# Strassen's seven products for two token chunks of an MLP's up-projection, and a down-projection by pairs of blocks

## The chip, the core and the metric

The kernel runs on one core of one Trainium2 chip. The metric is the device time of one execution in microseconds (us). Three runs of the kernel before took 1270.1, 1270.6 and 1271.15 us; the median is 1270.6.

## The reference

One layer of a hybrid decoder trunk for 1024 prompt tokens and 32 sample tokens of width 1024, in fp32. The first sub-layer (a mixer of gated spatial mixing, a gated linear recurrence and a convolution, between one input and one output projection) is not touched by the change. The second is a squared-ReLU MLP between two normalisations:

```python
h = _rmsnorm(x, g_pre_mlp[l]) * (1.0 + sc2) + sh2
y = jnp.square(jax.nn.relu(h @ w_up[l])) @ w_down[l]
x = x + gt2 * _rmsnorm(y, g_post_mlp[l])
```

`w_up` is 1024 x 4096 and `w_down` 4096 x 1024.

## The kernel before, in words

**Layout.** Features lie on the 128 partitions, tokens on the free axis. The 1056 tokens are `NCH` = 3 chunks of `CW` = 352 columns. `h2[c]` (filled by `after_mix`, L1487) holds the MLP's input of chunk c as 8 blocks of 128 features, each as a high and a low part in the fp32r format (hi is the rounded value, lo the rest). A weight block is split in the same way, so each product of a weight block with a block of tokens takes three matmuls: hi x hi, hi x lo, lo x hi (`product`, L344; `product8`, L354, does eight blocks of the contraction, 24 matmuls).

**The MLP.** The 32 output blocks of the up-projection are done four at a time, in eight steps j = 0 to 7 (loop at L1657). In a step, for each of four blocks f and three chunks, `up_group` (L1539) runs 24 matmuls into a PSUM tile, then ScalarE's ReLU (`relu`) and Square (`ah`, the high part), VectorE's square (`rsq`) and its residue (`al`, the low part). Then the down-projection of these four blocks: for each of eight output blocks m and three chunks `down_group` (L1554) runs 12 matmuls (four blocks of the contraction) into a PSUM tile, and VectorE adds it to the accumulator `acc`. So a step has 288 + 288 matmuls. In step 0 chunks 0 and 1 go through both projections before chunk 2, whose `h2` is ready last, and ScalarE copies instead of VectorE adding. In step 7 `last_down_group` (L1570) cuts the tokens into other groups, and `after_ff` (L1602) normalises and stores each.

**Weights.** `jobs` (from L283) lists the weight blocks of 512 KB in order of use. `fetch` (L300) allocates one of three `raw` tiles and issues its DMA on SyncE's queue; `split_next` (L307) has ScalarE write the high part (`whi`, 1024 columns) and VectorE the low part (`wlo`); `weights` (L336) hands out the oldest and splits ahead until two are ready. In the MLP there are three pairs of hi and lo tiles.

**Buffers.** PSUM has eight banks: three in the pool `pm` (L177; `pm_tile`, L365, all products so far) and five in `pb` (L178). SBUF tiles of 1056 columns come from `ep`, 17 of them (tag "e"; `full` and `e3`); eight are the accumulators, one per chunk and three m (the ninth piece is in `e2`), and eight the activations `ah` and `al` of a step. Each accumulator group of three for m = 6, 7 has a free third place.

**Order.** Every engine works through its own queue in the order in which the program issues. The order is written by hand: loops issue matmul groups, and `step(t)` (L224) between them lets generator tasks (`add_task`) issue the work of other stages, kind by kind, as long as a credit of time per engine (`Metered`, L85, with prices by operation) is left; `finish` (L249) issues what is left of all tasks.

Of the kernel before, what the change touches and what calls it, by code (L numbers as in the profile page):

```python
# [26 lines left out]
T_GROUP = 3.57  # L27
# [132 lines left out]
def trunk_kernel(ctx: ExitStack, tc: tile.TileContext, xT, cT, wada0, wada, vec, cst, msk, win, wout, wup,  # L160
# [5 lines left out]
    PE = Metered(nc.tensor, pe_price, credit, "pe", plan)  # L166
# [40 lines left out]
    def rs(name):  # L207
        return sp.tile([128, 512], F32, tag="rs", name=name)
# [40 lines left out]
    def finish():  # L249
        while any(queues.values()):  # L250
            step(T_GROUP / 2)
# [23 lines left out]
    jobs = []  # L275
# [10 lines left out]
    for cs in ((0, 1), (2,)):  # L286
        for f in range(4):
            jobs.append((wup[f], [128, 8, 128]))
        for m2 in range(4):
            jobs.append((wdn[0, m2], [128, 2, 4, 128]))  # L290
    for j in range(1, 8):
        for f in range(4):
            jobs.append((wup[4 * j + f], [128, 8, 128]))
        for m2 in range(4):
            jobs.append((wdn[j, m2], [128, 2, 4, 128]))

    homes = {}
    raws = []
# [1 line left out]
    def fetch():  # L300
        if jobs:
            src, shape = jobs.pop(0)
            raw = wp.tile(shape, F32, tag="raw", name="raw", bufs=3)
            SP.dma_start(out=raw, in_=src)
            raws.append((raw, shape))

    def split_next(later=False):  # L307
# [57 lines left out]
    def pm_tile():  # L365
        return pm.tile([128, CW], F32, tag="m", name="pmt")
# [231 lines left out]
    def hc(name):  # L598
        return hp.tile([128, 8, CW], F32, tag="c", name=name)
# [236 lines left out]
    def ch(t, c):  # L836
        return t[:, c * CW:(c + 1) * CW]
# [696 lines left out]


    acc = [None] * NCH
    homes[n_w[0] + len(raws) + len(jobs) - 1] = hc

    def up_group(w, a, c, j):  # L1539
        ps = pm_tile()  # L1540
        product8(ps, w, lambda k: (h2[c][0][:, k, :], h2[c][1][:, k, :]))
        ah, al = a
        t = rs("relu")[:, 0:CW]
        ACT.activation(out=t, in_=ps, func=AF.Relu)
        s2 = rs("rsq")[:, 0:CW]
        if j == 0:
            ACT.activation(out=s2, in_=t, func=AF.Square)
        else:
            DVE.tensor_tensor(out=s2, in0=t, in1=t, op=ALU.mult)
        ACT.activation(out=r(ch(ah, c)), in_=t, func=AF.Square)  # L1550
        DVE.tensor_tensor(out=r(ch(al, c)), in0=s2, in1=ch(ah, c), op=ALU.subtract)
        step(T_GROUP / STEPS)

    def down_group(w, mm, m, acts, c, j):  # L1554
        hi, lo = w
        ps = pm_tile()
        product(ps, (lambda k: hi[:, mm, k, :], lambda k: lo[:, mm, k, :]),
                lambda k: (ch(acts[k][0], c), ch(acts[k][1], c)), 4)
        a = acc[c][1](m)
        if j == 0:  # L1560
            ACT.copy(out=a, in_=ps)
        else:
            DVE.tensor_tensor(out=a, in0=a, in1=ps, op=ALU.add)
        step(T_GROUP / 2)


    CUT = 96
# [86 lines left out]

    put_off, rest = [], []

    for j in range(8):  # L1657
        acts = [(full("ah"), full("al")) for f in range(4)]
        if j == 0:
            for cs in ((0, 1), (2,)):  # L1660
                ws = {}
                for c in cs:
                    while h2[c] is None:
                        step(T_GROUP / 2)
                    for f in (3, 0, 1, 2) if c == 1 else range(4):
                        if c != 1:
                            ws[f] = weights()
                        up_group(ws[f], acts[f], c, j)
                if cs[0] == 0:
                    for c in range(NCH):  # L1670
                        acc[c] = blocks_of([(extra if (c, kk) == (2, 2) else e3)("acc") for kk in range(3)])
                for m2 in range(4):
                    w = weights()
                    for mm in range(2):
                        for c in cs:
                            down_group(w, mm, 2 * m2 + mm, acts, c, j)
            finish()
        else:
            for f in range(4):
# [3 lines left out]
        if j == 0:  # L1683
            continue
        if j < 7:
            for m2 in range(4):
                w = weights()
                for mm in range(2):
                    for c in range(NCH):
                        down_group(w, mm, 2 * m2 + mm, acts, c, j)  # L1690
        else:
            ws = []
            x1 = hc("x1")
            SP.dma_start(out=x1, in_=x1d[1])
            x1_last = hc("x1l")[:, 6:8, :]
            SP.dma_start(out=x1_last, in_=x1d[0, :, 6:8, :])
            tots = hc("tots")
            for g, parts in enumerate(GROUPS):
                tot = tots[:, 2 * g:2 * g + 2, :].rearrange("p a n -> p (a n)")[:, 0:sum(b - a for c, a, b in parts)]
                for m2 in range(4):  # L1700
                    if len(ws) < 4:
                        ws.append(weights())
                    for mm in range(2):
# [109 lines left out]
```

## Time and profile before

| | |
|---|---|
| runs, median (lowest to highest) | 1270.6 us (1270.1 to 1271.15) |
| profiled execution, own time | 1270.47 us |
| its span, first to last instruction | 1268.7 us |
| mean granted TensorE clock | 0.991 |
| TensorE busy | 1237.8 us, 8770 recorded matmuls |
| VectorE busy | 719.3 us |
| ScalarE busy | 488.4 us |
| GpSimd busy | 63.0 us |

Times in rows of the profile are in us unless a mean is marked ns. PE is TensorE, DVE VectorE, ACT ScalarE, POOL GpSimd, SP SyncE. A group's row gives what is written and read, the count, busy time and the mean of one in ns, and the idle time ahead of it with what ended that. All instructions are recorded at line L113, inside the wrapper that prices them, so groups are told apart by their tiles: `pmt` is a PSUM tile of a product, `h20hi` the high part of h2 in chunk 0, `ah`/`al` the activations, `whi`/`wlo` the split weights. Some matmul records are missing (of 768 matmuls with `ah` and `whi`, 744 are there), so counts of matmuls are taken from the code. The shown duration of a matmul (about 0.32 us) includes its pipeline; the pace is the distance between starts.

### The profile page before, as it was taken

What the parts mean: (1) busy time and instruction counts of PE and PEld (TensorE: products, weight loads), DVE (VectorE), ACT (ScalarE), POOL (GpSimd) and SP (SyncE); (2) the same over time, 40 slices, a digit from 0 to 9 for tenths busy, and PEclk for the clock granted to TensorE, in tenths of its full rate; (3) what the DMA queues carried; (4) which work ended last, traced back from release to release, by engine and by line L of the source; (5) the groups of instructions that cost most, each with busy time, mean ns of one, the idle gap of its engine ahead of it and who ended that gap; (6) DMA issues with size and microseconds to landing.
All of it is one profiled execution on the core that took longest, in us unless ns stands there. A gap on an engine that the chain in (4) does not pass through costs nothing.

```text
span 1268.7 us, 20674 instructions
## 1 busy us (share of the span) xinstructions
PE 1237.8 (98%) x8770; PEld 1194.8 (94%) x8770; DVE 719.3 (57%) x1096; ACT 488.4 (38%) x882; POOL 63.0 (5%) x107
## 2 busy tenths in 40 slices
PE   9999999999899999999999999999999999999995
PEld 7888889999899999899999999999999999999994
DVE  5799899688758768763333343333433333343366
ACT  6513464684764745555320321311311311312333
POOL 0000020211010011100000000000000000000001
PEclk9999999999999999999999999999999999999997
DMA  9568401111111467233211111111111110111218
GB/s 364 175 211 275 167 26 55 40 59 47 34 42 48 158 174 224 68 124 117 67 50 34 50 51 50 34 50 51 46 38 51 50 51 34 51 51 43 81 18 209
DMA packets 39245, 113.23 MB, mean 89 GB/s; under 512 B 9952, under 2 KB 12160, under 8 KB 39024
## 3 DMA queue, kind: packets, MB, share of 16 engines
q1 hardware_dynamic: 34832, 99.22, 22.8%
q0 software_dynamic: 4320, 12.68, 4.3%
q8 instruction: 69, 1.13, 0.3%
q14 instruction: 24, 0.20, 0.0%
HBM read 101.75 MB, written 10.14 MB: 88 GB/s over the span
## 4 chain that ended last, share of the span: by engine, by line
PE 81%; DVE 9%; ACT 6%; issue 1%; DMA 1%; POOL 1%; ACTq 0%; DVEq 0%; POOLq 0%
PE pmt L113 74%; PE stps L113 2%; PE adaps L113 1%; DVE acc L113 1%; DVE vf L113 1%; DMA o<-in_xT 1%; DVE q L113 1%; ACT vf L113 1%; ACT K L113 1%; PE sc L113 1%; DVE wlo L113 1%; PE pmt L736 1%; ACT whi L113 1%; DVE y L113 1%; DVE R L113 0%
## 5 line engine op out<-in xcount | busy, mean ns | idle before, releaser
L113 PE MATMUL pmt<-ah,whi 128*128 128x352 f32 (+2 forms) x744 | 241.4, 324 | 0.5 <-ACT acc L113 0.5
L113 PE MATMUL pmt<-al,whi 128*128 128x352 f32 (+2 forms) x744 | 240.3, 323 | 0.3
L113 PE MATMUL pmt<-ah,wlo 128*128 128x352 f32 (+2 forms) x744 | 240.2, 323 | 0.0
L113 ACT CAST whi<-raw 128x1024 fp32r<-128x1024 f32 (+2 forms) x113 | 114.2, 1013 | 262.2 <-PE pmt L113 260.1
L113 DVE TENSOR_TENSOR acc<-acc,pmt 128x352 f32<-128x352 f32 (+2 forms) x176 | 87.8, 503 | 167.6 <-PE pmt L113 167.6
L113 DVE TENSOR_TENSOR wlo<-raw,whi 128x1024 fp32r<-128x1024 f32 (+2 forms) x113 | 134.9, 1196 | 69.6 <-ACT whi L113 69.6
L113 DVE TENSOR_TENSOR rsq<-relu 128x352 f32<-128x352 f32 x84 | 44.2, 526 | 188.8 <-ACT relu L113 188.8
L113 PEld LDWEIGHTS pmt<-ah,whi 128*128 128x128 f32 x744 | 139.9, 188 | 2.0 <-ACT acc L113 0.8
L113 PEld LDWEIGHTS pmt<-al,whi 128*128 128x128 f32 x744 | 140.0, 188 | 1.6 <-DVE al L113 0.8
L113 PEld LDWEIGHTS pmt<-ah,wlo 128*128 128x128 f32 x744 | 140.0, 188 | 0.4
L113 ACT ACTIVATE relu<-pmt 128x352 f32<-128x352 f32 x96 | 44.6, 465 | 235.6 <-PE pmt L113 235.6
L113 PE MATMUL pmt<-h22hi,whi 128*128 128x352 f32 x256 | 82.5, 322 | 0.0
L113 PE MATMUL pmt<-h22hi,wlo 128*128 128x352 f32 x256 | 82.5, 322 | 0.0
L113 PE MATMUL pmt<-h22lo,whi 128*128 128x352 f32 x256 | 82.3, 322 | 0.0
L113 DVE SCALAR_TENSOR_TENSOR cva<-cvx,vec_t,cva 128x1024 f32<-128x1024 f32 x60 | 77.7, 1295 | 1.2
L113 PE MATMUL pmt<-h21lo,whi 128*128 128x352 f32 x232 | 74.7, 322 | 2.4 <-DVE h21lo L113 2.4
L113 PE MATMUL pmt<-h21hi,whi 128*128 128x352 f32 x232 | 75.2, 324 | 0.0
L113 PE MATMUL pmt<-h20hi,whi 128*128 128x352 f32 x232 | 74.8, 322 | 0.0
L113 PE MATMUL pmt<-h21hi,wlo 128*128 128x352 f32 x232 | 74.8, 322 | 0.0
L113 PE MATMUL pmt<-h20hi,wlo 128*128 128x352 f32 x232 | 74.7, 322 | 0.0
L113 PE MATMUL pmt<-h20lo,whi 128*128 128x352 f32 x232 | 74.6, 322 | 0.0
L113 DVE TENSOR_TENSOR al<-rsq,ah 128x352 fp32r<-128x352 f32 x96 | 50.4, 525 | 23.8 <-ACT ah L113 14.7
(361 smaller groups left out, 2694.8 us busy)
## 6 DMA issues: line engine op xcount, KB each, us to landing
rawada<-in_wada SPq DMA_DIRECT2D x48, 512.0 KB, 8.2
raw<-in_wup SPq DMA_DIRECT2D x36, 512.0 KB, 3.4
raw<-in_wdn SPq DMA_DIRECT2D x36, 512.0 KB, 3.4
raw<-in_win SPq DMA_DIRECT2D x22, 512.0 KB, 3.6
raw<-in_wout SPq DMA_DIRECT2D x20, 512.0 KB, 3.5
x<-in_xT SPq DMA_DIRECT2D x6, 528.0 KB, 6.9
o<-in_xT POOLq DMA_DIRECT2D x6, 528.0 KB, 7.3
x1d<-o POOLq DMA_DIRECT2D x6, 528.0 KB, 7.6
```

What stands on the lines that cost most here:

```text
L113: return f(**kw)
L736: nc.tensor.matmul(out=pss[m, c], lhsT=r(w_first[m][i % 2][:, k, :]), rhs=r(h[c][i // 2][:, k, :]), start=k == i == 0, stop=k == 7 and i == 2)
```

## The change

**Strassen (Winograd's form).** From the third pair of output blocks on (p = 2 is still plain, p = 3 to 15 are not), the up-projection works on pairs of output blocks. For chunks 0 and 1 the product of a 2 x 2 matrix of weight halves W(i, j) (i: half of the contraction, four blocks of 128; j: output block of the pair) with a 2 x 2 matrix of token halves is made by seven products of 12 matmuls (`part`, half depth) in place of eight. Chunk 2 keeps its 24 matmuls for each output block. This takes:

- sums of h, made once: `sums_of_h` in two parts (tasks during the end of step 0 and during p = 2) and `first_sum_of_h` (during the down-projection of p = 2, into the places of half of chunk 1's h2), each split into high and low part;
- sums of weights, for each pair: T12 and T34, two sums of 512 columns each, written by VectorE into PSUM tiles of `pb`, then cast by ScalarE and completed by VectorE (`begin_next`). Each is handled as one more weight block: a pair uses T12, W2, T34 and W1, and two blocks of down weights;
- three accumulators A, B, C in PSUM, of which partial values are taken between products (`pair_up`): three ScalarE copies and five VectorE additions with places in `acc`'s free thirds.

**Down-projection by pairs.** For p = 2 to 13 the down-projection follows each pair: 24 groups of six matmuls (two blocks of the contraction, the pair's second output block first, chunks in the order 2, 1, 0), each added to `acc` by VectorE (`down_pair`). A block of down weights now holds four m and two blocks of the contraction and is loaded by two DMAs. The last four blocks (pairs 14 and 15) go through `last_down_group` as before.

**Order of splits.** The splitting of weights is cut into `chores`, of which one is issued behind each product or group; `weight` hands out a block and begins the next.

```diff
-    for j in range(1, 8):
...
+    for p in range(2, 16):
+        for f in range(2):
+            jobs.append((wup[2 * p + f], [128, 8, 128]))
+        if p < 14:
+            for m4 in range(2):
+                jobs.append(([wdn[p // 2, 2 * m4 + i, :, :, p % 2 * 2:p % 2 * 2 + 2, :] for i in range(2)],
+                             [128, 4, 2, 128]))
+    for m2 in range(4):
+        jobs.append((wdn[7, m2], [128, 2, 4, 128]))
...
+    def sums_of_h(ks):
+        TT = DVE.tensor_tensor
+        (h0, l0), (h1, l1) = h2[0], h2[1]
+        for k in ks:
+            if k < 2:
+                ts = [full("s").rearrange("p (a n) -> p a n", n=CW) if k + i == 0 else extra("s") for i in range(2)]
+            else:
+                ts = [full("s").rearrange("p (a n) -> p a n", n=CW) for i in range(2)]
+            a, b, c, d = (*(spare(i) for i in range(3)), rstd_tile("d"))
+            TT(out=a, in0=h1[:, k, :], in1=l1[:, k, :], op=ALU.add)
+            TT(out=b, in0=h1[:, 4 + k, :], in1=l1[:, 4 + k, :], op=ALU.add)
+            yield
+            TT(out=c, in0=h0[:, k, :], in1=l0[:, k, :], op=ALU.add)
+            TT(out=b, in0=a, in1=b, op=ALU.add)
+            yield
+            TT(out=a, in0=c, in1=a, op=ALU.subtract)
+            TT(out=c, in0=b, in1=c, op=ALU.subtract)
+            yield
+            TT(out=d, in0=h0[:, 4 + k, :], in1=l0[:, 4 + k, :], op=ALU.add)
+            TT(out=d, in0=d, in1=c, op=ALU.subtract)
+            yield
+            at = [ts[i // 3][:, i % 3, :] for i in range(6)]
+            for i, x in enumerate((c, a, d)):
+                ACT.copy(out=r(at[2 * i]), in_=x)
+            yield 1.0
+            for i, x in enumerate((c, a, d)):
+                TT(out=r(at[2 * i + 1]), in0=x, in1=at[2 * i], op=ALU.subtract)
+                S[2 + i, k] = at[2 * i], at[2 * i + 1]
+            yield
...
+    KINDS = ["plain"] * 2 + (["T12", "W2", "T34", "W1"] + ["plain"] * 2) * 11 + ["T12", "W2", "T34", "W1"] * 2
...
+    def chore():
+        if chores:
+            chores.pop(0)()
+        while jobs and len(raws) + len(cur) < 3:
+            fetch()
...
+    def begin_next():
+        while chores:
+            chore()
+        kind = KINDS[begun[0]] if begun[0] < len(KINDS) else "plain"
+        begun[0] += 1
+        if kind == "plain":
+            if not raws:
+                fetch()
+            raw, shape = raws.pop(0)
+            cur["plain"] = raw
+            hi, lo = slot(shape)
+            split_of(hi, lo, raw, lambda: cur.pop("plain"))
+            ready.append((hi, lo))
+            return
+        W = lambda i, j: cur[j][:, 4 * i:4 * i + 4, :]
+        if kind in ("W1", "W2"):
+            hi, lo = slot([128, 8, 128])
+            split_of(hi, lo, cur[int(kind[1]) - 1], (lambda: cur.pop(0)) if kind == "W1" else None)
+            ready.append((hi, lo))
+            return
+        hi, lo = slot([128, 8, 128])
+        half = lambda t, i: t[:, 4 * i:4 * i + 4, :]
+        if kind == "T12":
+            while len(raws) < 2:
+                fetch()
+            cur[0], cur[1] = raws.pop(0)[0], raws.pop(0)[0]
+            ts = cur["T"] = [pb.tile([128, 4, 128], F32, tag="b", name="T") for i in range(2)]
+            DVE.tensor_tensor(out=ts[0], in0=W(0, 1), in1=W(0, 0), op=ALU.subtract)
+            DVE.tensor_tensor(out=ts[1], in0=W(1, 1), in1=ts[0], op=ALU.subtract)
+        else:
+            ts = [pb.tile([128, 4, 128], F32, tag="b", name="T"), cur.pop("T")[1]]
+            DVE.tensor_tensor(out=ts[0], in0=W(1, 1), in1=W(0, 1), op=ALU.subtract)
+            DVE.tensor_tensor(out=ts[1], in0=W(1, 0), in1=ts[1], op=ALU.subtract)
+            cur.pop(1)
+        def casts():
+            for i in range(2):
+                ACT.copy(out=r(half(hi, i)), in_=ts[i])
+        def rest():
+            for i in range(2):
+                DVE.tensor_tensor(out=r(half(lo, i)), in0=ts[i], in1=half(hi, i), op=ALU.subtract)
+        chores.extend((casts, rest))
+        ready.append((hi, lo))
+    def weight(more=True):
+        w = ready.pop(0)
+        if more:
+            begin_next()
+        return w
...
+        def part(ps, w, x, first=True):
+            hi, lo = w
+            for k in range(4):
+                xh, xl = x(k)
+                a, b = first and k == 0, k == 3
+                PE.matmul(out=ps, lhsT=r(hi[:, k, :]), rhs=r(xh), start=a, stop=False, skip_group_check=True)
+                PE.matmul(out=ps, lhsT=r(hi[:, k, :]), rhs=r(xl), start=False, stop=False, skip_group_check=True)
+                PE.matmul(out=ps, lhsT=r(lo[:, k, :]), rhs=r(xh), start=False, stop=b, skip_group_check=True)
...
+        def squares(*ts):
+            s2s = []
+            for t, f, c in ts:
+                s2s.append(rs("rsq")[:, 0:CW])
+                DVE.tensor_tensor(out=s2s[-1], in0=t, in1=t, op=ALU.mult)
+                ACT.activation(out=r(ch(acts[f][0], c)), in_=t, func=AF.Square)
+            for s2, (t, f, c) in zip(s2s, ts):
+                DVE.tensor_tensor(out=r(ch(acts[f][1], c)), in0=s2, in1=ch(acts[f][0], c), op=ALU.subtract)
...
+        p5 = p1 = spare(0)
+        p6, c12, c22 = spare(1), spare(2), rstd_tile("c22")
+        T12 = weight()
+        C = pm_tile()
+        part(C, half(T12, 0), sum_(1))
+        ACT.copy(out=p5, in_=C)
+        go_on()
+        B = pb.tile([128, CW], F32, tag="b", name="pmt2")
+        part(B, half(T12, 1), sum_(2))
+        ACT.copy(out=p6, in_=B)
+        go_on()
+        W2 = weight()
+        part(C, half(W2, 1), sum_(4), False)
+        add(c12, C, p6)
+        go_on()
+        A = pb.tile([128, CW], F32, tag="b", name="pmt2")
+        def third():
+            part(B, half(T34, 0), sum_(3), False)
+            add(c22, B, p5)
+            go_on()
+        def first():
+            part(A, half(W1, 0), of_h(0, 0))
+            add(c12, A, c12)
+            add(c22, A, c22)
+            ACT.copy(out=p1, in_=A)
+            squares((relu(c12, c12), 1, 0), (relu(c22, c22), 1, 1))
+            go_on()
+        def fourth():
+            part(B, half(T34, 1), of_h(1, 1), False)
+        def c21():
+            add(p1, B, p1)
+            squares((relu(p1, p1), 0, 1))
+        if last:
+            T34 = weight(False)
+            third()
+            chunk2(1, W2)
+            begin_next()
+            fourth()
+            go_on()
+            W1 = weight()
+            acts[0] = full("ah"), full("al")
+            first()
+            c21()
+            chunk2(0, W1)
+        else:
+            chunk2(1, W2)
+            T34 = weight()
+            third()
+            W1 = weight(False)
+            acts[0] = full("ah"), full("al")
+            first()
+            fourth()
+            begin_next()
+            c21()
+            go_on()
+            chunk2(0, W1)
+        part(A, half(W1, 1), of_h(0, 1), False)
+        squares((relu(A, rs("relu")[:, 0:CW]), 0, 0))
+        go_on()
...
+    def down_pair(w, mm, m, acts, c):
+        hi, lo = w
+        ps = pm_tile()
+        product(ps, (lambda k: hi[:, mm, 1 - k, :], lambda k: lo[:, mm, 1 - k, :]),
+                lambda k: (ch(acts[1 - k][0], c), ch(acts[1 - k][1], c)), 2)
+        a = acc[c][1](m)
+        DVE.tensor_tensor(out=a, in0=a, in1=ps, op=ALU.add)
+        step(T_GROUP / 4)
...
+    for p in range(2, 14):
+        acts = {}
+        if p == 2:
+            acts = {f: (full("ah"), full("al")) for f in range(2)}
+            add_task("conv", sums_of_h((2, 3)))
+            for f in range(2):
+                w = weight()
+                for c in range(NCH):
+                    up_group(w, acts[f], c, 1)
+                    chore()
+            add_task("conv", first_sum_of_h())
+        else:
+            pair_up(acts, False)
+        for m4 in range(2):
+            w = weight()
+            for mm in range(4):
+                for c in (2, 1, 0):
+                    down_pair(w, mm, 4 * m4 + mm, acts, c)
+                    chore()
+        if p == 2:
             finish()
-        else:
-            for f in range(4):
-                w = weights()
-                for c in range(NCH):
-                    up_group(w, acts[f], c, j)
-        if j == 0:
-            continue
-        if j < 7:
-            for m2 in range(4):
-                w = weights()
-                for mm in range(2):
-                    for c in range(NCH):
-                        down_group(w, mm, 2 * m2 + mm, acts, c, j)
-        else:
-            ws = []
-            x1 = hc("x1")
-            SP.dma_start(out=x1, in_=x1d[1])
-            x1_last = hc("x1l")[:, 6:8, :]
-            SP.dma_start(out=x1_last, in_=x1d[0, :, 6:8, :])
-            tots = hc("tots")
-            for g, parts in enumerate(GROUPS):
-                tot = tots[:, 2 * g:2 * g + 2, :].rearrange("p a n -> p (a n)")[:, 0:sum(b - a for c, a, b in parts)]
-                for m2 in range(4):
-                    if len(ws) < 4:
-                        ws.append(weights())
-                    for mm in range(2):
-                        last_down_group(ws[m2], mm, 2 * m2 + mm, acts, parts, tot)
-                add_task("first" if parts[0][0] == 1 else "recur", after_ff(parts, tot, parts[0][0] == 1))
+    acts, more = {}, {}
+    pair_up(acts, False)
+    pair_up(more, True)
...
```

More of the change, by code (lines that the diff above doesn't have):

```diff
@@ L303, in fetch @@
             raw = wp.tile(shape, F32, tag="raw", name="raw", bufs=3)
-            SP.dma_start(out=raw, in_=src)
+            if isinstance(src, list):
+                for i, x in enumerate(src):
+                    SP.dma_start(out=raw[:, 2 * i:2 * i + 2], in_=x)
+            else:
+                SP.dma_start(out=raw, in_=src)
             raws.append((raw, shape))
@@ L1536, in trunk_kernel @@
     acc = [None] * NCH
-    homes[n_w[0] + len(raws) + len(jobs) - 1] = hc
     def up_group(w, a, c, j):
@@ L1564, in down_group, with spare @@
         step(T_GROUP / 2)
+    S = {}
+    def spare(c):
+        return acc[c][1](8)
+    def sums_of_h(ks):
[27 more added lines that the diff above has]
+            yield
@@ new lines, in first_sum_of_h @@
+    def first_sum_of_h():
+        TT = DVE.tensor_tensor
+        h1, l1 = h2[1]
+        for k in range(4):
+            a, b = spare(k % 2), rstd_tile("d")
+            TT(out=a, in0=h1[:, k, :], in1=l1[:, k, :], op=ALU.add)
+            TT(out=b, in0=h1[:, 4 + k, :], in1=l1[:, 4 + k, :], op=ALU.add)
+            yield
+            TT(out=a, in0=a, in1=b, op=ALU.add)
+            ACT.copy(out=r(h1[:, k, :]), in_=a)
+            yield 0.5
+            TT(out=r(l1[:, k, :]), in0=a, in1=h1[:, k, :], op=ALU.subtract)
+            S[1, k] = h1[:, k, :], l1[:, k, :]
+            yield
@@ new lines, in trunk_kernel, with slot, split_of @@
+    chores = []
+    cur = {}
+    begun = [0]
+    KINDS = ["plain"] * 2 + (["T12", "W2", "T34", "W1"] + ["plain"] * 2) * 11 + ["T12", "W2", "T34", "W1"] * 2
+    def slot(shape):
+        n_w[0] += 1
+        pool = wpools[n_w[0] % len(wpools)]
+        return [pool.tile(shape, F32, tag=f"w{x}", name=f"w{x}") for x in ("hi", "lo")]
+    def chore():
[3 more added lines that the diff above has]
+            fetch()
+    def split_of(hi, lo, src, done=None):
+        ACT.copy(out=r(hi), in_=src)
+        def rest():
+            DVE.tensor_tensor(out=r(lo), in0=src, in1=hi, op=ALU.subtract)
+            if done:
+                done()
+        chores.append(rest)
@@ new lines, in begin_next, with rest @@
+    def begin_next():
[35 more added lines that the diff above has]
+                ACT.copy(out=r(half(hi, i)), in_=ts[i])
+        def rest():
+            for i in range(2):
+                DVE.tensor_tensor(out=r(half(lo, i)), in0=ts[i], in1=half(hi, i), op=ALU.subtract)
+        chores.extend((casts, rest))
+        ready.append((hi, lo))
@@ new lines, in weight, with pair_up, add, go_on @@
+    def weight(more=True):
[3 more added lines that the diff above has]
+        return w
+    def pair_up(acts, last):
+        half = lambda w, i: tuple(t[:, 4 * i:4 * i + 4, :] for t in w)
+        def part(ps, w, x, first=True):
+            hi, lo = w
+            for k in range(4):
+                xh, xl = x(k)
[3 more added lines that the diff above has]
+                PE.matmul(out=ps, lhsT=r(lo[:, k, :]), rhs=r(xh), start=False, stop=b, skip_group_check=True)
+        def add(out, a, b):
+            DVE.tensor_tensor(out=out, in0=a, in1=b, op=ALU.add)
+        def go_on():
+            step(T_GROUP / 2)
+            chore()
+        sum_ = lambda i: lambda k: S[i, k]
+        of_h = lambda c, i: lambda k: (h2[c][0][:, 4 * i + k, :], h2[c][1][:, 4 * i + k, :])
+        def relu(src, t):
+            ACT.activation(out=t, in_=src, func=AF.Relu)
+            return t
+        def squares(*ts):
[6 more added lines that the diff above has]
+                DVE.tensor_tensor(out=r(ch(acts[f][1], c)), in0=s2, in1=ch(acts[f][0], c), op=ALU.subtract)
+        def chunk2(f, w):
+            if f:
+                acts[f] = full("ah"), full("al")
+            ps = pm_tile()
+            part(ps, half(w, 0), of_h(2, 0))
+            go_on()
+            part(ps, half(w, 1), of_h(2, 1), False)
+            squares((relu(ps, rs("relu")[:, 0:CW]), f, 2))
+            go_on()
[53 more added lines that the diff above has]
+            c21()
+            go_on()
+            chunk2(0, W1)
+        part(A, half(W1, 1), of_h(0, 1), False)
+        squares((relu(A, rs("relu")[:, 0:CW]), 0, 0))
+        go_on()
@@ L1567, in trunk_kernel @@
+    def down_pair(w, mm, m, acts, c):
+        hi, lo = w
+        ps = pm_tile()
+        product(ps, (lambda k: hi[:, mm, 1 - k, :], lambda k: lo[:, mm, 1 - k, :]),
[3 more added lines that the diff above has]
+        step(T_GROUP / 4)
     CUT = 96
@@ new lines, in trunk_kernel @@
+    acts = [(full("ah"), full("al")) for f in range(4)]
+    for cs in ((0, 1), (2,)):
+        ws = {}
+        for c in cs:
+            while h2[c] is None:
+                step(T_GROUP / 2)
+            if c == 2:
+                add_task("conv", sums_of_h((0, 1)))
+            for f in (3, 0, 1, 2) if c == 1 else range(4):
+                if c != 1:
+                    ws[f] = weights()
+                up_group(ws[f], acts[f], c, 0)
+        if cs[0] == 0:
+            for c in range(NCH):
+                acc[c] = blocks_of([(extra if (c, kk) == (2, 2) else e3)("acc") for kk in range(3)])
+        for m2 in range(4):
+            w = weights()
+            for mm in range(2):
+                for c in cs:
+                    down_group(w, mm, 2 * m2 + mm, acts, c, 0)
@@ new lines, in trunk_kernel @@
+    finish()
+    for p in range(2, 14):
[5 more added lines that the diff above has]
+                w = weight()
+                for c in range(NCH):
+                    up_group(w, acts[f], c, 1)
+                    chore()
+            add_task("conv", first_sum_of_h())
+        else:
+            pair_up(acts, False)
[4 more added lines that the diff above has]
+                    down_pair(w, mm, 4 * m4 + mm, acts, c)
+                    chore()
+        if p == 2:
+            finish()
@@ new lines, in trunk_kernel @@
+    acts, more = {}, {}
+    pair_up(acts, False)
+    pair_up(more, True)
+    while chores:
+        chore()
+    acts.update({2 + f: a for f, a in more.items()})
+    homes[n_w[0] + len(raws) + len(jobs) - 1] = hc
+    ws = []
+    x1 = hc("x1")
+    SP.dma_start(out=x1, in_=x1d[1])
+    x1_last = hc("x1l")[:, 6:8, :]
+    SP.dma_start(out=x1_last, in_=x1d[0, :, 6:8, :])
+    tots = hc("tots")
+    for g, parts in enumerate(GROUPS):
+        tot = tots[:, 2 * g:2 * g + 2, :].rearrange("p a n -> p (a n)")[:, 0:sum(b - a for c, a, b in parts)]
+        for m2 in range(4):
+            if len(ws) < 4:
+                ws.append(weights())
+            for mm in range(2):
+                last_down_group(ws[m2], mm, 2 * m2 + mm, acts, parts, tot)
+        add_task("first" if parts[0][0] == 1 else "recur", after_ff(parts, tot, parts[0][0] == 1))
```

23 lines of the change are left out of this document (removed).

## The prediction

> **What bounds the kernel now.** I read the profile's page first, then the chain of waits, then TensorE's waits behind 560 us, then a table of windows, and only then single instructions.
>
> ```profile
> span 1268.7 us, 20674 instructions
> ...
> PE 1237.8 (98%) x8770; PEld 1194.8 (94%) x8770; DVE 719.3 (57%) x1096; ACT 488.4 (38%) x882; POOL 63.0 (5%) x107
> ...
> PE   9999999999899999999999999999999999999995
> ...
> DVE  5799899688758768763333343333433333343366
> ...
> PEclk9999999999999999999999999999999999999997
> ```
>
> TensorE is full in nearly every slice. VectorE (DVE) is at 80% or more at times in the first half and at 30 to 40% in the second, which is the MLP that the change touches. The profiled execution took 1270.47 us: the span of 1268.7 and 1.8 around it. It lies 0.1 under the median of the runs shown (1270.6), so the sum below is made against 1270.47.
>
> ```profile
> 588.69 614.04 PE pmt L113 x3830
> ```
>
> ```profile
> PE sums L113 <- DVE tots L113: 1.5, 1, 1.5
> PE stps L113 <- DVE diag L113: 1.3, 2, 1.0
> PE pmt L113 <- ACT acc L113: 0.5, 1, 0.5
> ```
>
> ```profile
> 500.00:530.00 30.00, 27.61 (x168) 26.69 (x167) 22.82 (x34) 16.81 (x33) 0.55 (x1) 1.00 0.34 129
> ...
> 576.00:592.00 16.00, 15.84 (x97) 15.31 (x96) 7.00 (x8) 9.60 (x18) 0.00 (x0) 1.00 0.38 124
> 592.00:607.00 15.00, 15.00 (x96) 15.00 (x95) 4.91 (x4) 6.54 (x11) 0.00 (x0) 1.00 0.41 140
> 800.00:1000.00 200.00, 200.00 (x1250) 200.00 (x1249) 75.73 (x123) 44.61 (x74) 0.00 (x0) 1.00 0.14 46
> ...
> 1250.00:1262.00 12.00, 3.64 (x28) 2.67 (x26) 10.96 (x22) 3.96 (x11) 2.94 (x3) 0.73 1.05 234
> ```
>
> The chain runs for 614 us through matmuls alone, and behind 560 us TensorE waits 0.5 us for anything inside the blocks. In the window from 800 to 1000 (columns: TensorE, weight loads, VectorE, ScalarE, GpSimd, then the clock) TensorE is busy for 200 of 200 us at clock 1.00, VectorE for 75.7. So in this stage time is the number of matmuls times their pace, and a removed matmul counts in full, as long as no new wait on TensorE appears.
>
> **Matmuls removed.** The pace, from two ScalarE rows that each follow an up-projection group of 24 matmuls, eight groups apart:
>
> ```profile
> 802.63 0.47 ACT L113 ACTIVATE relu<-pmt 128x352 f32<-128x352 f32 x1 [1.88 <-PE pmt L113]
> ...
> 833.30 0.47 ACT L113 ACTIVATE relu<-pmt 128x352 f32<-128x352 f32 x1 [2.84 <-PE pmt L113]
> ```
>
> 30.67 us / 8 / 24 = 0.160 us. A pair of output blocks over chunks 0 and 1 took 2 x 2 x 24 = 96 matmuls; seven products of 12 are 84. Pairs p = 3 to 15 do this, 13 of them: 13 x 12 = 156 matmuls, 156 x 0.160 = 24.9 us. Chunk 2, the pair p = 2 and all down-projections keep their matmul counts (24 groups of 6 for a pair, where a block of four had 24 of 12).
> The Trainium skill, "TensorE: Matmul & The Clock Gate", section Back-to-back issue gap, gives N/2.4 + 2.5 ns, for 352 columns an estimate of 149 ns; by it the removal would be worth 23.3 us, and since the trace has 160 the measurement decides.
>
> **What VectorE gets instead.** Durations of the steady blocks (640 to 1200 us), and two rows of the whole run for 512 columns:
>
> ```profile
> L113 DVE TENSOR_TENSOR acc<-acc,pmt 128x352 f32<-128x352 f32 x144 | 74.9, 520 | 159.5 <-PE pmt L113 159.5
> ...
> L113 DVE TENSOR_TENSOR wlo<-raw,whi 128x1024 fp32r<-128x1024 f32 x49 | 60.1, 1226 | 17.1 <-ACT whi L113 17.1
> L113 ACT CAST whi<-raw 128x1024 fp32r<-128x1024 f32 x48 | 50.0, 1043 | 246.2 <-PE pmt L113 246.2
> L113 DVE TENSOR_TENSOR rsq<-relu 128x352 f32<-128x352 f32 x74 | 38.9, 526 | 166.1 <-ACT relu L113 166.1
> ```
>
> ```profile
> L113 DVE TENSOR_TENSOR s0t<-s0t,uss 128x512 f32<-128x512 f32 x4 | 2.7, 686 | 13.4 <-POOL s0t L113 13.4
> ...
> L113 DVE TENSOR_TENSOR wlo<-raw,whi 128x512 fp32r<-128x512 f32 x2 | 1.3, 684 | 0.0
> ```
>
> Per pair: 24 accumulations x 0.52 = 12.5 (a block of four needed 24, so these double), four raw splits x 1.23 = 4.9, four weight sums T x 0.69 = 2.7, their four low halves x 0.69 = 2.7, five combining additions x 0.52 = 2.6, twelve squares and residues x 0.53 = 6.3: 31.7 us. TensorE's time for a pair is 84 + 48 + 144 = 276 matmuls x 0.160 = 44.1 us. VectorE goes from 38% to 72%: not the bound on average. ScalarE adds two T casts' worth (2 x 1.04) and three copies of 0.47, and stays far below half. Inside the up-projection half I find each result ready before its reader: the copies and additions on accumulators A, B and C run under the next product of 12 matmuls (1.92 us), and the T34 halves are asked for at 9.6 us of the pair and ready by about 5 (sums issued at its start, 1.4 us; casts behind the first product, 1.2 us; low halves, 1.3 us). If that cover failed, the price would be one or two 0.5 us operations a pair.
>
> **Where it does not stay hidden: the start of each down-projection.** The pair's last product A closes just before, the next pair's T12 sums are issued at the first weight(), ahead of the first accumulation, and VectorE works in order. These rows give the latencies (the matmul is the first one of the group behind the one that the relu reads):
>
> ```profile
> 802.43 0.32 PE L113 MATMUL pmt<-h21hi,whi 128*128 128x352 f32 x1
> ```
>
> ```profile
> 803.13 0.53 DVE L113 TENSOR_TENSOR rsq<-relu 128x352 f32<-128x352 f32 x1 [1.12 <-ACT relu L113]
> 803.77 0.52 DVE L113 TENSOR_TENSOR al<-rsq,ah 128x352 fp32r<-128x352 f32 x1
> ...
> 835.27 1.23 DVE L113 TENSOR_TENSOR wlo<-raw,whi 128x1024 fp32r<-128x1024 f32 x1 [0.32 <-ACT whi L113]
> 836.41 0.51 DVE L113 TENSOR_TENSOR acc<-acc,pmt 128x352 f32<-128x352 f32 x1
> ```
>
> ```profile
> 561.47 0.43 PE L113 MATMUL pmt<-ah,whi 128*128 128x352 f32 x1 [0.49 <-ACT acc L113]
> 561.74 0.32 PE L113 MATMUL pmt<-al,whi 128*128 128x352 f32 x1
> ```
>
> ```profile
> 560.98 0.80 ACT L113 COPY acc<-pmt 128x352 f32<-128x352 f32 x2
> ```
>
> Count from the moment A closes (802.43 in the rows). The relu starts at 0.20, the square on VectorE at 0.70, the residue ends at 1.86. An independent operation starts 0.09 before its predecessor's end (836.41 against 836.50), a dependent one 0.1 behind it (803.77 against 803.66). So the first T sum runs from 1.77 to 2.46, the second, which reads the first, from 2.57 to 3.26, and the first accumulation from 3.17 to 3.69. Down groups now last 6 x 0.160 = 0.96 us, and three PSUM buffers serve them: the fourth group wants the first one's buffer at 2.88. It gets it at about 3.7, one 0.8 us wait; a waiting matmul starts some 0.05 behind its releaser (two copies take 0.80 from 560.98, so the first ends near 561.42; the matmul starts at 561.47) and loses 0.11 more at restart (561.74 - 561.47 = 0.27 in place of 0.16). About 1.0 us. The rest of the down-projection queues behind that matmul and is late by as much; no other engine needs it sooner. Behind it VectorE still has the two T low halves (1.4 us) between accumulations, which just fits the next two buffers (add 0 to 0.2), then gains 0.4 us a group. Before, groups were 1.92 us, and the three buffers gave 5.8 us: that is why no such wait shows.
> No row has VectorE writing PSUM, as the T sums do. From below take the 352-column price (0.53 each, wait about 0.7), from above the 1024-column one (1.23 each, wait about 2.1); I take 0.69, since the s0t row reads PSUM at 512 columns for the same price as SBUF. This happens for p = 3 to 13, eleven times: 11 x 1.0 = 11.0 us (8 to 23).
> The Trainium skill, "Perfetto Trace Analysis", section Optimization Strategy, takes the same gap repeating on the engine that should be saturated as a sign of too little SBUF or PSUM for the next tile; no row of before shows such a gap.
>
> **The preparation.** The block sums of h cost 4 x 11 + 4 x 4 = 60 VectorE operations of 0.53 us, 32 us in all, half of the first part in j = 0 for chunk 2, where VectorE has 31 - 11.9 = 19 us free (the windows from 576 to 607) against 11.7 needed: 0.5 us allowed. The rest falls into p = 2, whose 288 matmuls last 46 us: 6 x 1.06 for squares, 4 x 1.23, 24 x 0.52, T12 with 2.8, 38 sums x 0.53 = 20.1, together 46.6. Operations overlap by 0.09, so it is just full. Here the down-projection also begins with chunk 2, whose last relu was computed just before: the first matmul waits 1.2 us for the high part and the second until about 1.9. So 1.9 + about 2 for bursts and for the first T product that waits for the last sums: 4.0 us (2 to 8).
> The last pair's T34 and the late second half of the last weights: 0.5 us.
>
> **At nothing.** Down weights arrive by two DMAs of 256 KB in place of one.
>
> ```profile
> raw<-in_wdn SPq DMA_DIRECT2D x36, 512.0 KB, 3.4
> ```
>
> Each is issued a split or more ahead, over 5 us before ScalarE reads it; if that cover went, ScalarE would queue a cast of 1 us behind a landing of 3.4. Only raw loads use SP's queue there.
>
> **Sum.** 1270.47 - 24.9 + 11.0 + 4.0 + 0.5 = 1261.1; I say 1261.0. By the bounds: 1270.5 - 24.9 + 8 + 2 = 1255.6 and 1270.5 - 24.9 + 23 + 8 + 1 = 1277.6; the upper one needs all three at once, so the forecast's own range is 1255 to 1267.
>
> **Rivals.**
> Full saving: the wait at the down-projection's start is 0.2 us or less, because VectorE's queue moves up by 0.8 us (shorter sums, or a buffer more than I count). Only the preparation is then paid: 1270.5 - 24.9 + 2.2 + 2 = about 1250. For it: TensorE hides everything today. Against it: three buffers and the order of issue are in the code, and the chain's durations are rows.
> Slower: VectorE's sums into PSUM cost as much as the 1.23 us row or more, so that every down-projection starts 2.1 us late and, with VectorE near 77% (31.7 + 4 x 0.54 of 44.1 us), p = 2 costs 8: 1270.5 - 24.9 + 23 + 8 = 1276.6. It decides against the change from (24.9 - 4.5) / 11 = 1.85 us of wait a pair on, that is from sums of 1.1 us each. Against it: 686 ns for the PSUM reader.
> Clock: the repeated short gaps lower the granted clock. The window with 8.4 of 12 us idle has 0.73; but 500 to 530, with a gap of 2.4 us in all, has 1.00. At 0.95 over 13 pairs (13 x 44.1 / 0.95) it would add 30 us: 1291. The Trainium skill, "TensorE: Matmul & The Clock Gate", section A second HAM failure mode: psum-queue depth-cycling, describes micro-idles between groups that throttle the clock; the 500 to 530 row does not bear it out.
> That the change does not do what it says I exclude: the seven calls of part() are there.
>
> **How the numbers follow.** Forecast 0.68, full saving 0.21, slower 0.08, clock 0.03. The range of 1247 to 1268 takes in the forecast and the full saving and leaves out the last two and the forecast's upper tail. About 0.2%, 2.5 us, can be told from no change, so faster means under 1268: the forecast without its tail and the full saving, 0.87; same 0.04, from the tail; slower 0.09.
>
> **What would show it.** 156 matmuls fewer at 0.160 us; VectorE near 70% in windows of the steady pairs at clock 1.00; in TensorE's waits a new row, matmul on VectorE's accumulation, about eleven times near 0.8 us, at the fourth group of each down-projection, and a longer stretch around p = 2. No such row, or a row many times as frequent, would make the walk wrong; T sums far from 0.69 us its price.

## The result, and the profile after

The changed kernel takes 1260.31 us (median of four runs, 1258.88 to 1263.86) against 1270.88 for the kernel before on the same chip (the three runs given above and one of 1271.88): ratio 0.9921, 95% interval 0.9896 to 0.9945, 10.6 us faster. The forecast was 1261.0.

The profiled execution is the slowest of the four (1263.86 us, span 1262.1). These are the lines of its page that answer to those of before:

```profile
span 1262.1 us, 20853 instructions
...
PE 1221.9 (97%) x8614; PEld 1171.4 (93%) x8614; DVE 902.0 (71%) x1469; ACT 533.6 (42%) x989; POOL 63.0 (5%) x107
...
DVE  5799889688658768866686657657666765765766
...
PEclk9999999999999999999999999999999999999998
```

8770 - 8614 = 156 recorded matmuls fewer, and VectorE is now busy for 50 to 80% of each slice of the second half, where it was mostly 30 to 40%. The granted clock stays at 0.9 or more up to the last slice, as before. TensorE's waits behind 540 us (total, times, longest), and two windows with the columns as before:

```profile
PE pmt L113 <- DVE acc L113: 5.8, 12, 0.5
PE pmt L113 <- ACT ah L113: 1.7, 2, 1.1
...
PE pmt L113 <- DVE al L113: 1.3, 3, 0.6
```

```profile
610.00:660.00 50.00, 48.51 (x300) 47.64 (x299) 39.39 (x77) 16.05 (x31) 0.00 (x0) 1.00 0.10 33
...
705.00:1130.00 425.00, 420.43 (x2592) 415.06 (x2591) 279.42 (x496) 122.68 (x223) 0.00 (x0) 1.00 0.15 48
```

Before, TensorE waited for nothing inside the blocks but 0.5 us. Now there is one wait for each down-projection on an accumulation, eleven of 0.5 us from p = 3 on and one of 0.17 in p = 2. The chain of waits shows the beat; each of these pieces of matmuls begins with the matmul that waited:

```profile
679.35 41.83 PE pmt L113 x258
724.67 41.81 PE pmt L113 x258
769.98 41.83 PE pmt L113 x258
```

A pair lasts 45.3 us. One of these waits from close by, first on TensorE, then on VectorE:

```profile
675.68 0.32 PE L113 MATMUL pmt<-ah,whi 128*128 128x352 f32 x1
...
678.52 0.32 PE L113 MATMUL pmt<-ah,wlo 128*128 128x352 f32 x1
679.35 0.43 PE L113 MATMUL pmt<-ah,whi 128*128 128x352 f32 x1 [0.51 <-DVE acc L113]
679.62 0.32 PE L113 MATMUL pmt<-al,whi 128*128 128x352 f32 x1
```

```profile
676.37 0.53 DVE L113 TENSOR_TENSOR rsq<-relu 128x352 f32<-128x352 f32 x1
677.00 0.53 DVE L113 TENSOR_TENSOR al<-rsq,ah 128x352 fp32r<-128x352 f32 x1
677.44 0.70 DVE L113 TENSOR_TENSOR T<-raw 128x512 f32<-128x512 f32 x1
678.17 0.69 DVE L113 TENSOR_TENSOR T<-raw,T 128x512 f32<-128x512 f32 x1
678.78 0.94 DVE L113 TENSOR_TENSOR acc<-acc,pmt 128x352 f32<-128x352 f32 x2
```

The first matmul of the down-projection starts at 675.68, three groups of six follow, and the fourth could start at 678.68. VectorE does square, residue and the two T12 sums first; its first accumulation starts at 678.78, and the fourth group starts right behind it at 679.35, 0.67 us late, with 0.27 in place of 0.16 to the next matmul.

**Where the time went.** Step 0's chunk 2 comes to its up-projection 2.9 us later in this profile than in that of before (574.10 and 571.19), in code that is the same in both. The last wait ahead of it ends at 564.37 in this profile and at 561.47 in that of before. From there to the end it takes 1262.1 - 564.4 = 697.7 us against 1268.7 - 561.5 = 707.2: 9.5 us less. The stages of that: 156 matmuls at 0.160, -25.0; eleven pairs of 45.3 us in place of 276 x 0.160 = 44.2, +12; p = 2 with 48.5 us (606.03 to 654.50) in place of 288 x 0.160 = 46.1, +2.4; step 0, +0.5; from the start of the last down-projection to the end, 66.7 us (from 1195.35) in place of 66.1 (from 1202.56), +0.6.

### The profile page after: what moved, and what is told of

It is laid out like the page before. It is cut to its first block, busy times and chain, and to the rows that moved or that the text cites. A ratio compares the mean times of both kernels' runs of the same rounds, so it can differ in the third digit from the quotient of the medians.

```text
span 1262.1 us, 20853 instructions
## 1 busy us (share of the span) xinstructions
PE 1221.9 (97%) x8614; PEld 1171.4 (93%) x8614; DVE 902.0 (71%) x1469; ACT 533.6 (42%) x989; POOL 63.0 (5%) x107
## 4 chain that ended last, share of the span: by engine, by line
PE 78%; DVE 11%; ACT 6%; DMA 3%; issue 2%; POOL 0%; SPq 0%; DVEq 0%; ACTq 0%
PE pmt L113 71%; DVE acc L113 2%; PE adaps L113 1%; DMA rawada<-in_wada 1%; DVE T L113 1%; PE pmt L744 1%; DVE wlo L113 1%; DMA o<-in_xT 1%; ACT K L113 1%; ACT vf L113 1%; DVE q L113 1%; PE sc L113 1%; DVE rsq L113 1%; ACT relu L113 1%; PE ob L113 1%
## 5 line engine op out<-in xcount | busy, mean ns | idle before, releaser
L113 PE MATMUL pmt<-ah,whi 128*128 128x352 f32 (+2 forms) x744 | 244.0, 328 | 7.9 <-DVE acc L113 5.8
L113 DVE TENSOR_TENSOR acc<-acc,pmt 128x352 f32<-128x352 f32 (+1 forms) x320 | 158.5, 510 | 91.8 <-PE pmt L113 91.6
L113 ACT COPY acc<-pmt 128x352 f32<-128x352 f32 x63 | 28.4, 452 | 196.7 <-PE pmt L113 161.8
L113 PE MATMUL pmt<-s,whi 128*128 128x352 f32 x312 | 75.6, 324 | 0.0
L113 ACT ACTIVATE relu<-pmt 128x352 f32<-128x352 f32 x57 | 26.4, 463 | 104.2 <-PE pmt L113 101.3
L113 PE MATMUL pmt<-h1hi,whi 128*128 128x352 f32 x168 | 55.7, 332 | 2.6 <-DVE gq L113 2.6
L113 PE MATMUL pmt<-h2hi,whi 128*128 128x352 f32 x168 | 56.7, 337 | 0.0
L113 PE MATMUL pmt<-h0hi,whi 128*128 128x352 f32 x168 | 55.5, 330 | 0.8 <-DVE gq L113 0.8
L113 PEld LDWEIGHTS pmt<-s,whi 128*128 128x128 f32 x312 | 54.5, 188 | 0.0
L113 DVE TENSOR_TENSOR rsq<-relu 128x352 f32<-128x352 f32 x45 | 23.5, 523 | 43.0 <-ACT relu L113 41.8
```

Source lines behind the costliest of these rows:

```text
L113: return f(**kw)
```

## The experiments

My theory is the forecast's: the first accumulation of each down-projection stands on VectorE behind two T12 sums, and three PSUM buffers are too few to wait for it. Rival A: the 1.1 us a pair are no wait on that, but a slower pace or VectorE's load as such. Rival B: wherever the sums are put, they delay something by as much.

### The changed kernel again

No edit.

> The changed kernel itself, once more beside the others. Its four runs spread from 1258.9 to 1263.9 us, while the kernel before spreads from 1270.1 to 1271.9; in the profiled one 2.9 us of that had come before the MLP, in code that the change does not touch. Expected: a median of 1258 to 1261, a pair's period of 45.3 us, and a stage from the first pair to the end as in the first profile.

1260.32 us (1259.79 to 1263.65, five runs on another chip; ratio 0.9937, 0.9923 to 0.9951). The chain has 721.10 and 766.41, a period of 45.3 us. In this profile the last wait ahead of step 0's chunk 2 ends at 560.80, and from there to the end it takes 1258.6 - 560.8 = 697.8 us, as in the first profile (697.7). The result repeats, and the 2.9 us ahead of the MLP do not belong to the change.

### Six buffers

```diff
-        ps = pm_tile()
+        ps = pb.tile([128, CW], F32, tag="b", name="pmt2") if mm % 2 else pm_tile()
```

> Every second set of three down-projection groups takes its PSUM tile from the other pool, so that six buffers serve the groups in place of three; order and work stay. Theory (the fourth group waits for the first accumulation, which stands behind the T12 sums on VectorE): the 0.67 us wait and its restart go, a pair's period falls from 45.3 to 44.2 to 44.4, eleven pairs give 10 to 12 us, and the kernel comes to 1247 to 1251. Rival A (the 1.1 us a pair are a slower pace of the matmuls, or VectorE's load as such): period and time stay within 2 us of the changed kernel.

1250.34 us (1248.31 to 1250.79), ratio 0.9848 (0.9835 to 0.9862): 10.0 us under the changed kernel measured beside it. The wait on `acc` is gone from TensorE's list, and the chain runs from p = 2 to the last pair through matmuls alone:

```profile
626.12 548.40 PE pmt L113 x3407
```

VectorE's T12 sums, which stand at the start of each down-projection, show the period:

```profile
760.97 0.69 DVE L113 TENSOR_TENSOR T<-raw 128x512 f32<-128x512 f32 x1
...
805.38 0.69 DVE L113 TENSOR_TENSOR T<-raw 128x512 f32<-128x512 f32 x1
```

The one before starts at 716.55: a period of 44.4 us. 45.3 - 44.4 = 0.9, times eleven is 10. Rival A falls, since work and load are unchanged.

### The sums behind the first accumulations

```diff
-            DVE.tensor_tensor(out=ts[0], in0=W(0, 1), in1=W(0, 0), op=ALU.subtract)
-            DVE.tensor_tensor(out=ts[1], in0=W(1, 1), in1=ts[0], op=ALU.subtract)
+            w00, w01, w11 = W(0, 0), W(0, 1), W(1, 1)
+            chores.append(lambda: DVE.tensor_tensor(out=ts[0], in0=w01, in1=w00, op=ALU.subtract))
+            chores.append(lambda: DVE.tensor_tensor(out=ts[1], in0=w11, in1=ts[0], op=ALU.subtract))
```

> Three buffers as in the changed kernel, but the two T12 sums are issued behind the first and the second accumulation of the down-projection in place of ahead of all. Theory: the first accumulation comes 1.3 us earlier, the fourth group finds its buffer free, period 44.2 to 44.5, time 1248 to 1252. Rival A, VectorE's load as such: VectorE does the same work between the same ends, so nothing moves by more than 2 us. Rival B, the wait only moves: the sums delay a later accumulation just as much, and the period stays near 45.3.

1250.59 us (1249.79 to 1253.2), ratio 0.9857 (0.9842 to 0.9872), with three buffers. TensorE's waits:

```profile
PE pmt L113 <- DVE acc L113: 0.3, 2, 0.2
```

5.8 us in twelve waits have become 0.3 in two, and the T12 sums start 44.4 us apart (674.56, 718.97). Rival B falls too: spread between the accumulations, the same sums delay nothing. So either the order on VectorE or the number of buffers is enough to undo the wait; it takes both to make it.

### The sums twice

```diff
             DVE.tensor_tensor(out=ts[0], in0=W(0, 1), in1=W(0, 0), op=ALU.subtract)
             DVE.tensor_tensor(out=ts[1], in0=W(1, 1), in1=ts[0], op=ALU.subtract)
+            DVE.tensor_tensor(out=ts[0], in0=W(0, 1), in1=W(0, 0), op=ALU.subtract)
+            DVE.tensor_tensor(out=ts[1], in0=W(1, 1), in1=ts[0], op=ALU.subtract)
```

> The two T12 sums are computed twice in a row at their old place, 1.3 us more on VectorE ahead of the first accumulation. Theory: each of the eleven pairs waits 1.25 to 1.3 us longer, period 46.6, time 1271 to 1276, so slower than before the change or equal to it. Rival A (pace or load): VectorE goes from 68% to 71% in the pairs and TensorE hides it: under 3 us.

1290.33 us (1286.54 to 1293.88), ratio 1.017 (1.0152 to 1.0188): 30 us more than the changed kernel and 14 beyond what I had expected at most. The direction is the theory's, the size is not. The chain shows two kinds of pairs, and the windows that begin with a waiting matmul show what differs (the last column but two is the clock):

```profile
677.02 41.84 PE pmt L113 x258
723.81 43.22 PE pmt L113 x258
772.00 41.83 PE pmt L113 x258
818.79 43.22 PE pmt L113 x258
```

```profile
677.00:719.00 42.00, 41.98 (x261) 41.84 (x262) 26.75 (x48) 11.47 (x22) 0.00 (x0) 1.00 0.12 38
...
723.80:767.10 43.30, 43.29 (x260) 43.29 (x261) 26.77 (x48) 11.40 (x22) 0.00 (x0) 0.96 0.12 37
```

Four of the ten periods in the chain are 46.8 us, 1.5 more than in the changed kernel, about what the theory has (1.3). Six are 48.2, and in these the clock is 0.96. From close by:

```profile
721.51 0.32 PE L113 MATMUL pmt<-ah,wlo 128*128 128x352 f32 x1
723.81 0.46 PE L113 MATMUL pmt<-ah,whi 128*128 128x352 f32 x1 [1.98 <-DVE acc L113]
724.08 0.49 PE L113 MATMUL pmt<-al,whi 128*128 128x352 f32 x1
724.37 0.50 PE L113 MATMUL pmt<-ah,wlo 128*128 128x352 f32 x1
724.66 0.50 PE L113 MATMUL pmt<-ah,whi 128*128 128x352 f32 x1
```

Behind a gap of 723.81 - 721.67 = 2.14 us (721.67 is the last start, 721.51, and one pace) matmuls follow each other at 0.29 us in place of 0.16 for some 3.7 us, up to 727.55, and the pair loses another 1.4 us. That is the clock rival of the prediction, in a kernel with a longer gap than the change has. The gaps of the longer and of the shorter pairs are alike (2.12 to 2.14 us), so what decides between them stays open. The profiled execution is the shortest of the five; the other four, 1288.37 to 1293.88 us, have granted clocks of 0.980 to 0.984 against its 0.985, so more of their pairs may be long ones. Their pairs are not on record.

### One sum twice, and half a sum more

```diff
             DVE.tensor_tensor(out=ts[0], in0=W(0, 1), in1=W(0, 0), op=ALU.subtract)
+            DVE.tensor_tensor(out=ts[0], in0=W(0, 1), in1=W(0, 0), op=ALU.subtract)
             DVE.tensor_tensor(out=ts[1], in0=W(1, 1), in1=ts[0], op=ALU.subtract)
```

> Only the first of the two T12 sums is computed twice: 0.6 us more on VectorE ahead of the first accumulation, half of what the doubled pair of sums added. There six of ten pairs lasted 48.2 us and four 46.8, and the longer ones show 0.29 us from matmul to matmul for some time behind a gap of 2.14 us in place of 0.16. Theory, wait plus a clock that falls only behind a longer gap: all pairs last 45.9 to 46.0, clock 1.00 throughout, time 1267 to 1270. Rival, any gap above a microsecond can lower the clock: some pairs last about 47.4, time above 1271.

1270.66 us (1268.22 to 1274.22, ten runs), ratio 1.0003 (0.9991 to 1.0015). The chain:

```profile
679.22 41.83 PE pmt L113 x258
725.28 41.81 PE pmt L113 x258
771.31 41.83 PE pmt L113 x258
```

All pairs last 46.05 us, 0.73 more than in the changed kernel, at clock 1.00. Eleven times 0.73 is 8; the total is 0.7 above what I had expected, since p = 2, where VectorE is full, loses more as well: from the wait in step 0 to the one in the first pair's down-projection it takes 679.22 - 589.53 = 89.7 us, in the changed kernel 679.35 - 592.11 = 87.2. This kernel has the whole saving of 156 matmuls and no gain: a further 0.6 us on VectorE at this place is the break-even point.

The second kernel adds a further sum over half of the columns.

```diff
+            DVE.tensor_tensor(out=ts[0][:, 0:2, :], in0=W(0, 1)[:, 0:2, :], in1=W(0, 0)[:, 0:2, :], op=ALU.subtract)
```

> Between the two kernels with repeated sums: the first T12 sum is computed once more in full and once more for half of its columns, about 0.95 us more on VectorE ahead of the first accumulation. Gaps on TensorE of 1.42 us left the clock at 1.00, gaps of 2.14 us were followed by a slower stretch in six of ten pairs. Theory of the wait: gaps of about 1.75 us and pairs of 46.4 us. For the clock: if all pairs last 46.4, the bound lies above 1.75 us; if some last about 47.8, below.

1276.67 us (one run). The gap on TensorE:

```profile
724.31 0.32 PE L113 MATMUL pmt<-ah,wlo 128*128 128x352 f32 x1
726.34 0.43 PE L113 MATMUL pmt<-ah,whi 128*128 128x352 f32 x1 [1.71 <-DVE acc L113]
```

726.34 - 724.47 = 1.87 us, and every period in the chain is 46.5 us. The clock did not fall behind 1.87 us in these ten pairs, and did behind 2.14 us in six of ten.

### The order of chunks at p = 2

```diff
-                for c in (2, 1, 0):
+                for c in (0, 1, 2) if p == 2 else (2, 1, 0):
```

> The changed kernel with only the order of chunks at p = 2 turned to 0, 1, 2. Theory: TensorE's two waits there (1.08 and 0.23 us, on ah and al) are gone from its list, and p = 2, 48.45 us long in the changed kernel, lasts about 46.9. Rival: the T12 sums stand ahead of the first accumulation here too, so that a wait of 0.5 to 0.8 us on it takes their place, and p = 2 lasts 47.5 to 48.

1259.83 us (one run). From the wait in step 0 to the wait in the first pair's down-projection it takes 675.95 - 588.71 = 87.24 us, in the changed kernel's second profile 675.78 - 588.53 = 87.25: nothing is gained. TensorE's waits:

```profile
PE pmt L113 <- DVE acc L113: 6.8, 14, 0.6
```

The waits on `ah` and `al` at this place are gone, and two more on accumulations (629.34 and 632.27, 0.6 and 0.4 us) have taken their place. The rival of the expectation is right for this kernel.

### The three edits together

Six buffers, the order at p = 2, and in the last pair the addition of c21 ahead of the remaining low half (`go_on` issues the next chore, here that low half; `first(False)` leaves its `go_on` out):

```diff
-            first()
+            first(False)
             c21()
+            go_on()
             chunk2(0, W1)
```

> Six buffers as before; at p = 2 the down-projection takes the chunks in the order 0, 1, 2, so that the group whose ReLU came last is not first; in the last pair the addition of c21 is issued ahead of the remaining low half of the down weights. Theory: over the 1250.3 us of six buffers alone the 1.3 us of waits at the start of p = 2's down-projection and about 1 us at the start of the last one go: 1247 to 1249. Rival: both waits are made up for behind (VectorE is full in p = 2 anyway), and the time stays at 1250 to 1251.

1247.7 us (1245.58 to 1248.14), ratio 0.982 (0.9806 to 0.9833). With six buffers the order at p = 2 does pay: from the wait in step 0 to the first pair's T34 sums there are 647.60 - 586.85 = 60.8 us against 62.6 with six buffers alone, and the chain of matmuls runs from 586.85 to the last pair. TensorE's waits:

```profile
PE pmt L113 <- DVE al L113: 1.9, 2, 1.3
```

The other half of the expectation failed: 1.3 us at the start of the last down-projection remain, now on `al`, because the low half (1.2 us) stands ahead of the last two squares. It was put behind them in one more kernel; the edit is against the kernel with three edits:

```diff
             c21()
-            go_on()
+            held = chores[:]
+            chores.clear()
             chunk2(0, W1)
...
         squares((relu(A, rs("relu")[:, 0:CW]), 0, 0))
+        if last:
+            chores.extend(held)
         go_on()
```

> As the kernel with all three edits (1247.7 us), but in the last pair the low half of the down weights (1.2 us on VectorE) is issued only behind the last two squares, not ahead of them. There it still stood in front of them, and TensorE waited 1.27 us for al at the start of the last down-projection. Theory: that wait goes or falls under 0.3 us, and the kernel comes to 1246 to 1247. Rival: the low half is then late for the last down-projection itself and as much is lost there; 1247.5 to 1249.

1247.19 us (1246.9 to 1247.51), ratio 0.982 (0.9805 to 0.9836). The list has no wait at that place any more, and 0.6 us on `al` in step 0 remain:

```profile
PE pmt L113 <- DVE al L113: 0.6, 1, 0.6
```

The total cannot be told from the kernel with three edits, and the expectation (1246 to 1247) is missed by 0.2. These two are the fastest versions: 13 us under the change, 22 to 23 under the kernel before.

### Pairs without Strassen

All up-projections plain (2 x 3 x 24 matmuls for a pair, no sums), the down-projection by pairs with six buffers and the chunks in the order 0, 1, 2. Core of the edit:

```diff
-    KINDS = ["plain"] * 2 + (["T12", "W2", "T34", "W1"] + ["plain"] * 2) * 11 + ["T12", "W2", "T34", "W1"] * 2
+    KINDS = []
...
-            pair_up(acts, False)
+        acts = plain_up()
...
```

> No Strassen: pairs 2 to 15 are plain up-projections of 2 x 3 x 24 matmuls, no sums of h or of weights, six buffers, the down-projection by pairs with the chunks in the order 0, 1, 2. Theory: the doubled accumulations hide, so the kernel is like the one before, 1268 to 1272 us, and the seven products are worth some 20 us against six buffers with Strassen (1250.3): 156 matmuls at 0.160 less the preparation. Rival: groups of six matmuls cost TensorE something of their own (more starts of groups, more waits), 1275 or more; then the pairs were part of what the gain lost.

1269.12 us (1267.09 to 1270.57, eleven runs), ratio 0.9993 (0.9984 to 1.0002). TensorE waits for nothing in the blocks:

```profile
586.03 613.29 PE pmt L113 x3830
```

Cutting the down-projection into groups of six matmuls with twice the accumulations is free by itself, at least with six buffers. Between this kernel and the one with three edits lie 21.4 us, which is what the seven products bring here when hardly anything waits for them, out of the 25.0 us that the removed matmuls took.

## Why the prediction was right, point by point

**The sum.** The forecast lies 0.7 us from the measured time, closer than its terms. It took off 24.9 us and added 15.5; the stages show 25.0 and 15.5, but the pairs cost 12 and not 11, and the preparation 2.9 and not 4.0. That these two errors cancel is luck.

**Matmuls removed.** 156 at 0.160 us: the records have 156 fewer, and the pace is nearly unchanged (44.4 / 276 = 0.161 in pairs without the wait).

**The wait at the start of the down-projection.** This was the decisive step, and it is shown: more buffers undo it (10.0 us), another order undoes it (9.7), more work at the place makes it longer. The price of a T sum was taken as 0.69 us and is 0.69; the first accumulation was put 3.17 us behind A and starts 3.10 behind it (the second, dependent sum starts 0.03 and not 0.1 behind the first). By the two removals the wait is worth 0.9 us a pair, where I had 1.0. The list of waits shows 0.5 and not the 0.8 I had announced: it counts from the modelled end of a matmul, 0.32 us behind its start, while time is lost from 0.16 on; and it has twelve entries, not eleven. The remaining 0.2 us of a pair's 45.3 appear where the list shows no wait: in the pair from 679.35 on, two more matmuls are followed by the next after 0.27 us in place of 0.16 (681.40 and 721.64), in a pair with six buffers one (759.84). What holds these matmuls up I did not try.

**Preparation.** Taken as 4.0 us, measured as 2.4 in p = 2 and 0.5 in step 0. The mechanism was half right. The wait for the last ReLU at p = 2 is there (1.08 and 0.23 us), but the second half of my sum, two microseconds for bursts, came to less; and turning the order alone does not help, because the T12 sums then make the next wait.

**VectorE's load.** 72% forecast, 279.42 / 425 = 66% measured. A pair lasts 45.3 us and not 44.1, which makes it 31.7 / 45.3 = 70%. The rest is that the rows' durations overlap by 0.09 us, which I had used in the walk and not in the load.

**The last pair.** 0.5 us forecast; from the start of the last down-projection to the end it takes 0.6 longer than before. That the two agree is luck. The waits at that start, on `ah` and `al` (0.59 and 0.42 us), are others than those I named: chunk 2's ReLU in the last pair stands on ScalarE behind the one for c21, which waits for VectorE.

**The rivals.** Full saving did not happen, and is 10 us away by one line. Slower by costly sums did not: its break-even, 1.85 us of wait a pair or 0.85 more than forecast, lies about where it was put: in the kernel with one sum twice the pairs last 46.05 us, 1.85 more than 44.2, and it came out at 1.0003. The clock stayed at 1.00 through all pairs, as the row from 500 to 530 had it, but the mechanism exists at a gap 1.5 us longer; had I known its bound, its chance would have rested on the gap's length and not on one row. The repeated gap of the page "Perfetto Trace Analysis" in the Trainium skill, section Optimization Strategy, is what the trace shows, 0.67 us eleven times, and buffers were the cure it implies, though the order on VectorE cures it as well.

## What to carry to other kernels

When a matmul-bound stage gives up matmuls for vector work, its average load says little: walk the vector queue at the one place where buffers are short, and ask what stands ahead of the instruction that frees the next buffer. Halving the depth of a group also halves the time for which a given number of buffers covers a late evacuation, 5.8 us before and 2.9 after, so buffers or order must change with it (here three buffers cost 0.9 us a pair, and six or another order none). A wait taken away can leave the next one at the same place, as at p = 2: try the two edits together before dropping one.

## What the runs showed of the hardware that I had not expected

TensorE's clock fell behind a gap of 2.14 us (start-to-start less one pace) in six of ten cases (the pairs' clock is 0.96 there), and then matmuls of 352 columns came every 0.29 us in place of 0.16 and cost 1.4 us more a time; behind gaps of 0.67, 1.42 and 1.87 us it did not fall in any pair of the chain. The Trainium skill, "TensorE: Matmul & The Clock Gate", section A second HAM failure mode: psum-queue depth-cycling, has short idle times between groups of matmuls make the clock alternate between a half and a full rate; in the changed kernel with 0.67 us the trace does not agree, in the kernel with 2.14 us it does, with 0.29 us from matmul to matmul in place of 0.16.
